# A hybrid HGRN2 / S5 layer on one core: projections of the unnormalised input, norms applied when an accumulator is emptied, head-norm chain at another priority, one reciprocal to four tokens

## The chip, the cores and the metric

The kernel runs on one core of one Trainium2 chip. The metric is the device time of one execution in microseconds; a kernel's time is the median of its timed runs. The engines are named as in the profile: PE (TensorE, matmul), PEld (its weight loads), DVE (VectorE), ACT (ScalarE), POOL (GpSimd), SP (the engine that issues most DMAs). L101 is line 101 of the kernel.

## The reference

One layer over 16 learned meta tokens and 256 tokens of the input (272 rows) of width 2048, in float32:

```python
xn = rmsnorm(h, norm_mix)                  # y = h * rsqrt(mean(h*h) + eps) * g, per row (token)
proj = xn @ w_in                           # 2048 x 5120
q, f_logit, i_in, g_out, u = split(proj)   # five times 1024 columns
# HGRN2, 8 heads, state 128x128, in chunkwise form:
f = lb + (1 - lb) * sigmoid(f_logit);  k = (1 - lb) * sigmoid(-f_logit);  q = silu(q);  v = i_in
S_t = diag(f_t) S_{t-1} + k_t v_t^T;       o_t = S_t^T q_t
o_hg = rmsnorm_per_head(o) * gain * silu(g_out)
# S5, 64 groups of 16 channels, 64 complex states each, diagonal recurrence along the tokens:
y = C (scan of ab * state + B u) + d * u;  y = gelu(y);  y = y * sigmoid(y @ w_glu + b_glu);  o_s5 = rmsnorm(y)
h = h + concat(o_hg, o_s5) @ w_out
# gated MLP of width 5632 with a causal convolution (width 3) on the gate branch, then a final rmsnorm
h = h + (silu(conv(n @ w_gate)) * (n @ w_up)) @ w_down     # n = rmsnorm(h, norm_ffn)
```

The factor rsqrt(mean(h*h) + eps) of the first norm belongs to a token, so it can be applied to the row of the input or to the finished row of the projection.

## The kernel before

**Layout.** Activations lie transposed: channels on the 128 partitions, tokens along the free axis. `xT` holds the input as 16 tiles of 128 x 272. Weights come in units of 1024 x 256, 1 MB by one DMA, in three rotating buffers `raw`; a unit consists of two halves, each 128 x 1024.

**Split products.** Every float32 product is made of rounded parts. For a weight half, ACT casts `whi` (L169) and DVE subtracts `wlo = raw - whi` (the helper `tt`, L92), each in three rotating buffers. The input is split likewise into `xh` and `xl`. `mm3` issues three matmuls for each pair of tiles: hi by high part (L193), hi by low part (L194), lo by high part (L195). A half of a projection serves 24 matmuls, and a chunk of 256 output columns takes 4 halves, 96 matmuls, into two accumulators `acc` (m = 0 and 1). Accumulators rotate through three PSUM buffers, so that the second accumulator of a chunk needs the first one of the chunk before to have been emptied.

**Stages.** (1) The head of the program: input rows arrive, PE transposes them into `xT`, ACT and DVE sum their squares (`row_rs`, L274), a small chain makes the factor of each token (`sqrt_rs`, L264), PE spreads it over the partitions (`rbp`, L298), and it lands in `rbs` (L307, L310). Then for each of the 16 tiles DVE forms `xn = xT * gm * rbs` (L101), ACT casts `xh` (L340), and DVE subtracts `xl`. The first two weight units are split in eight pieces of 512 columns, six of the subtracts on POOL; ten matmuls into `wps` (L312, 20 records in the trace) keep PE busy until the first `xh` is there. (2) 20 chunks of projections in the order u0 h0 u1 h1 u2 h2 u3 h3 g0 g1 g2 g3. `u` feeds the S5 part: per chunk two tiles `j`, each with its own weights (`s5_b`: B times small factors on POOL, copies `eb` and `cp` on ACT) and two scan passes (`s5_scan`: a rotation table W of six `stt`, products P, a sum on POOL, a scan, products, the sum `xo`), then a sum of products on PE (`yps`) and a GELU. `h` is three chunks (f, q, i) and the recurrence of two heads (`hg_group`, `hg_cross`); the tile `f` and later scratch of this recurrence share the one buffer `PP`. `g` is the output gate. (3) The head norms: squares of `oT` are summed by PE (`hps`, L862), a chain on DVE (`rsqrt`, then `hr`) makes eight factors, PE spreads each (`bps`, L893), and DVE multiplies, ACT casts `mh`, DVE subtracts `ml`, all beside the four chunks of `w_glu`. (4) `w_out` in 16 units, then the gated MLP and the last norm.

**Order.** A scheduler orders the instructions of each engine when the program is built: it takes what is ready in its own reckoning by priority (`pri`): splits of weights first (-4), then the emptying of accumulators (-3), then HGRN2 (-2), the rest by their place in the code, matmuls of weights last (+1). The result is one fixed list per engine; at run time each engine goes through its list in order, and an instruction that waits holds up all behind it.

## Time and profile before

| | |
|---|---|
| median of 3 runs (lowest, highest) | 1227.13 us (1224.62, 1233.77) |
| profiled execution: time, span | 1229.55 us, 1227.8 us |
| mean granted clock of PE | 0.993 |
| PE busy | 1205.0 us, 98% of the span |
| DVE busy | 892.9 us, 73% |
| ACT busy | 623.6 us, 51% |
| POOL busy | 83.2 us, 7% |
| moved by DMA | 210.66 MB, 172 GB/s |

The profiled execution lies 2.4 us above the median of the runs, and 1.75 us of its time lies outside the span. All times below that have a decimal place are microseconds from the start of this span. The page's list of busy tenths shows DVE at 9 from about 100 to 340 us and at 5 to 7 afterwards. A row of the trace's stages gives, after the stretch and its length, the busy time (and instructions) of PE, PEld, DVE, ACT and POOL, then the granted clock of PE, the busy share of the DMA engines and their GB/s. A row of the timeline gives start, duration, engine, line, operation, output <- inputs and shape, and in brackets the idle time ahead of it and what ended that. Engines are pipelined: DVE instructions that follow each other start about 0.08 us before the one ahead has ended, so a series costs its durations less 0.08 each.

### The profile page before, as it was taken

The page shows a single profiled execution, that of the slowest core. Times are in us where ns is not written, and L with a number is a line of the kernel's source. Part 1 is how long each engine was busy: PE and PEld are TensorE (multiplying, and loading weights), DVE is VectorE, ACT ScalarE, POOL GpSimd, SP SyncE. Part 2 cuts the span into 40 slices and gives each one's busy share as a digit, 9 for nine tenths or more (in the row PEclk, how much of TensorE's full clock was granted, in tenths as well). Part 3 has the DMA queues.
Part 4 walks back from the last instruction along what each step waited for, and adds up shares of the span by engine and source line. Part 5 has one row for each costly group of instructions (what it writes and reads, how often), then busy time and mean ns, then how long its engine had stood idle before and what let it go on. Part 6 is the DMA issues. An engine that isn't in the chain of part 4 may idle for free.

```text
span 1227.8 us, 21177 instructions
## 1 busy us (share of the span) xinstructions
PE 1205.0 (98%) x8531; PEld 1108.1 (90%) x8531; DVE 892.9 (73%) x1516; ACT 623.6 (51%) x1066; POOL 83.2 (7%) x102
## 2 busy tenths in 40 slices
PE   7989999999999999999999999999999999999997
PEld 6989999999989999999999999999999788888885
DVE  8988999999979778766666666765766555555554
ACT  6756667675655466444444444444443344444444
POOL 5231222111100000000000000000000000000000
PEclk9999999999999999999999999999999999999998
DMA  8544344434445555555655556565555545555552
GB/s 255 153 127 143 116 139 128 127 109 138 146 135 175 185 185 172 189 189 177 198 174 190 188 180 194 175 195 182 181 196 172 206 172 204 179 199 199 181 213 93
DMA packets 176289, 210.66 MB, mean 172 GB/s; under 512 B 14772, under 2 KB 168879, under 8 KB 170415
## 3 DMA queue, kind: packets, MB, share of 16 engines
q1 hardware_dynamic: 175871, 209.22, 52.4%
q8 instruction: 67, 1.10, 0.4%
q14 instruction: 31, 0.25, 0.1%
q0 software_dynamic: 320, 0.09, 0.0%
HBM read 206.08 MB, written 2.10 MB: 170 GB/s over the span
## 4 chain that ended last, share of the span: by engine, by line
PE 95%; DVE 2%; issue 1%; DMA 1%; ACT 1%; SPq 0%; POOL 0%; DVEq 0%; ACTq 0%; POOLq 0%
PE ua L976 13%; PE acc L193 10%; PE acc L194 9%; PE acc L195 9%; PE ga L193 7%; PE ga L195 7%; PE ga L194 7%; PE ua L982 7%; PE d L1047 7%; PE d L1049 7%; PE d L1048 7%; PE bu L623 1%; PE lps L753 1%; DVE xn L101 1%; DMA x<-in_x 0%
## 5 line engine op out<-in xcount | busy, mean ns | idle before, releaser
L92 DVE TENSOR_TENSOR wlo<-raw,whi 128x1024 fp32r<-128x1024 f32 (+1 forms) x376 | 462.0, 1229 | 288.6 <-ACT whi L169 238.7
L169 ACT CAST whi<-raw 128x1024 fp32r<-128x1024 f32 (+1 forms) x382 | 397.7, 1042 | 483.1 <-PE ga L194 157.4
L193 PE MATMUL ga<-fh,whi 128*128 128x258 f32 x704 | 198.9, 283 | 0.0
L195 PE MATMUL ga<-fh,wlo 128*128 128x258 f32 x704 | 198.1, 282 | 0.0
L194 PE MATMUL ga<-fl,whi 128*128 128x258 f32 x704 | 198.1, 282 | 0.0
L193 PE MATMUL acc<-xh,whi 128*128 128x272 f32 (+1 forms) x640 | 185.0, 293 | 3.1 <-ACT whi L169 3.1
L194 PE MATMUL acc<-xl,whi 128*128 128x272 f32 (+1 forms) x640 | 185.3, 291 | 1.9 <-DVE xl L92 1.9
L195 PE MATMUL acc<-xh,wlo 128*128 128x272 f32 (+1 forms) x640 | 183.2, 292 | 0.0
L194 PEld LDWEIGHTS ga<-fl,whi 128*128 128x128 f32 x704 | 133.6, 190 | 0.0
L193 PEld LDWEIGHTS ga<-fh,whi 128*128 128x128 f32 x704 | 133.1, 189 | 0.0
L195 PEld LDWEIGHTS ga<-fh,wlo 128*128 128x128 f32 x704 | 132.5, 189 | 0.0
L1048 PE MATMUL d<-whi,al 128*128 128x512 f32 x328 | 128.1, 391 | 0.0
L1047 PE MATMUL d<-whi,ah 128*128 128x512 f32 x328 | 127.4, 393 | 0.3 <-ACT ah L1040 0.3
L193 PEld LDWEIGHTS acc<-xh,whi 128*128 128x128 f32 x640 | 120.1, 189 | 7.1 <-ACT whi L169 3.3
L194 PEld LDWEIGHTS acc<-xl,whi 128*128 128x128 f32 x640 | 120.8, 189 | 4.7 <-DVE xl L92 2.8
L195 PEld LDWEIGHTS acc<-xh,wlo 128*128 128x128 f32 x640 | 119.6, 189 | 2.4 <-issue 1.0
L1049 PE MATMUL d<-wlo,ah 128*128 128x512 f32 x328 | 114.4, 390 | 0.0
L976 PE MATMUL ua<-fcxh,whi 128*128 128x512 f32 x352 | 96.6, 395 | 0.0
L976 PE MATMUL ua<-fcxl,whi 128*128 128x512 f32 x352 | 96.1, 394 | 0.0
L1047 PEld LDWEIGHTS d<-whi,ah 128*128 128x128 f32 x328 | 61.9, 189 | 13.3 <-ACT ah L1040 0.5
L1048 PEld LDWEIGHTS d<-whi,al 128*128 128x128 f32 x328 | 62.0, 189 | 12.9
L1049 PEld LDWEIGHTS d<-wlo,ah 128*128 128x128 f32 x328 | 61.9, 189 | 13.0
(417 smaller groups left out, 1897.7 us busy)
## 6 DMA issues: line engine op xcount, KB each, us to landing
raw<-in_w_ffn_gate SPq DMA_DIRECT2D x44, 1024.0 KB, 5.1
raw<-in_w_ffn_up SPq DMA_DIRECT2D x44, 1024.0 KB, 5.1
...
```

Of the source, the lines that this page charges most:

```text
L92: eng.tensor_tensor(out=dst, in0=a, in1=b, op=op)
L101: dve.scalar_tensor_tensor(out=dst, in0=a, scalar=s, in1=b, op0=op0, op1=op1, **kw)
L169: act.copy(out=hi[:, c], in_=raw[:, hf, c])
L193: pe.matmul(accs[m], lh, xh[:, n0:n1], start=first, stop=False)
L194: pe.matmul(accs[m], lh, xl[:, n0:n1], start=False, stop=False)
L195: pe.matmul(accs[m], ll, xh[:, n0:n1], start=False, stop=end)
L623: return pe.matmul(bus[i][:, ri], bt[h, 2 * ri + q0 // 2], R[h, q0 // 2], start=True, stop=True)
L976: pe.matmul(accs[m].rearrange("p a n -> p (a n)"), hi[:, k * 256 + m * 128:k * 256 + m * 128 + 128], c.rearrange("p a n -> p (a n)"), star ...
L982: pe.matmul(accs[m][:, 0], lo[:, k * 256 + m * 128:k * 256 + m * 128 + 128], c[:, 0], start=False, stop=(kt == KD - 1), skip_group_check=True)
L1047: pe.matmul(dps[t][n], ah[:, tk], hi, start=False, stop=False, skip_group_check=True)
L1048: pe.matmul(dps[t][n], al[:, tk], hi, start=False, stop=False, skip_group_check=True)
L1049: pe.matmul(dps[t][n], ah[:, tk], lo, start=False, stop=end, skip_group_check=True)
```

## The change

- The projections take the input without its row factor. `xh` is ACT's `xT * gm` rounded (one activation with a scale per partition), `xl` is one DVE instruction, `xT * gm - xh`. `xn` is gone. `gm` no longer carries the factor -0.5, and `norm_mix` is loaded ahead of the input.
- The first two weight units and the 16 tiles are split in eight steps, each tied to follow the one before: `whi` and `wlo` of 512 columns, then two tiles. All eight subtracts are on DVE; the ten matmuls into `wps` are gone.
- The row factors are made as before, most of it at a later priority, into three columns `rcol`; they are spread by PE after the chunk u0 into a PSUM buffer of the accumulators, and ACT copies them to `rbs`.
- The row factor is applied when an accumulator is emptied: `ysb` (was a copy on ACT), `f`, `q` and `g` by a `tt` on DVE with `rbs`, followed by sigmoids from SBUF; `v` by ACT's copy with a scale.
- In `hg_group`, the reciprocal of 512 elements per partition is replaced by one of 128 (one to a block of four tokens), three `tt` of 128, one of 384 and an ACT copy.
- In `s5_scan`, the axes of `P` are stored in another order, and the sum is made in place instead of in a tile `m`.
- `c_kinds(1)`, small work for the S5 part, stands in chunk u2 instead of after u1.
- The chain of the head norms (`hrs`, `hr`, `ht`) has an offset of -3 within its -2, which sets it ahead of the splits of weights.

```diff
     early = []
-    deps = []
+    units = []
 
     def wunit(src):
         with pri(-4):
-            return wsplit(early.pop(0), (dve, pool), 2, deps.pop(0)) if early else wsplit(wload(src))
-
-    def wsplit(raw, eng=(dve, dve), parts=1, dep=None):
+            return units.pop(0) if units else wsplit(wload(src))
+
+    def wsplit(raw):
         res = []
-        n = 1024 // parts
         for hf in range(2):
             hi = wsp.tile([128, 1024], F32R, tag="whi", name="whi")
             lo = wsp.tile([128, 1024], F32R, tag="wlo", name="wlo")
-            if dep is not None and dep[hf] is not None:
-
-                act.copy(out=hi[:, 0:1], in_=dep[hf])
-            for i in range(parts):
-                c = slice(i * n, (i + 1) * n)
-                act.copy(out=hi[:, c], in_=raw[:, hf, c])
-                tt(lo[:, c], raw[:, hf, c], hi[:, c].bitcast(F32), SUB, eng[max(hf, i)])
+            act.copy(out=hi, in_=raw[:, hf])
+            tt(lo, raw[:, hf], hi.bitcast(F32), SUB)
             res.append((hi, lo))
...
-    rbp = [pmm.tile([128, NM + 128], F32, tag="mm", name=f"rbp{b}") for b in range(2)]
-    rbs = xin.tile([128, T], F32, name="rbs")
+    rbs = s5p.tile([128, T], F32, name="rbs")
...
-    rm = row_rs(xm, NM, 1, "rm")
-    rb = [None, None]
+    gm = prm.tile([128, KD], F32, name="gm")
+    gps = ptp.tile([128, KD], F32, tag="tp", name="gps")
+    pe.transpose(gps, nrow, ident[0:KD, 0:KD])
+    dve.tensor_copy(out=gm, in_=gps)
-        rb[b] = row_rs(xt[b], 128, 2, f"rb{b}")
-        if b == 0:
-            spread(rm, NM, rbp[0][:, 0:NM])
-            spread(rb[0], 128, rbp[0][:, NM:])
-            act.copy(out=rbs[:, 0:NM + 128], in_=rbp[0])
-        else:
-            spread(rb[1], 128, rbp[1][:, 0:128])
-            dve.tensor_copy(out=rbs[:, NM + 128:T], in_=rbp[1][:, 0:128])
-            for _ in range(NWARM2):
-                pe.matmul(wps, ident, rbs[:, NM + 128:T], start=True, stop=True)
...
-            gm = prm.tile([128, KD], F32, name="gm")
-            gps = ptp.tile([128, KD], F32, tag="tp", name="gps")
-            pe.transpose(gps, nrow, ident[0:KD, 0:KD])
-            ts(gm, gps, -0.5, MUL)
+    last = None
+    for p in range(8):
+        u, hf, c = p // 4, p // 2 % 2, slice(512 * (p % 2), 512 * (p % 2) + 512)
+        if p % 4 == 0:
+            units.append([])
+        if p % 2 == 0:
+            units[u].append([wsp.tile([128, 1024], F32R, tag=t, name=t) for t in ("whi", "wlo")])
+        hi, lo = units[u][hf]
+        raw = early[u][:, hf, c]
+
+        def split():
+            i = act.copy(out=hi[:, c], in_=raw)
+            tt(lo[:, c], raw, hi[:, c].bitcast(F32), SUB)
+            return i.ins
+
+        if last is None:
+            wi = split()
+        else:
+            with tc.issue_after(last):
+                wi = split()
+        with tc.issue_after(wi):
+            for kt in (2 * p, 2 * p + 1):
+                last = act.activation(out=xh[:, kt], in_=xT[:, kt], func=AF.Identity, scale=gm[:, kt:kt + 1]).ins
+                stt(xl[:, kt], xT[:, kt], gm[:, kt:kt + 1], xh[:, kt].bitcast(F32), MUL, SUB)
+
+    rcol = s5p.tile([128, 3], F32, name="rcol")
+    rb = [row_rs(xt[0], 128, 2, "rb0")]
+    with pri(0.5):
+        rb += [row_rs(xt[1], 128, 2, "rb1"), row_rs(xm, NM, 1, "rm")]
+    for i, n in enumerate((128, 128, NM)):
+        ts(rcol[:n, i:i + 1], rb[i], -0.5, MUL)
...
-    for kt in range(KD):
-        xn = xin.tile([128, T], F32, tag="xn", name="xn", bufs=4)
-        stt(xn, xT[:, kt], gm[:, kt:kt + 1], rbs, MUL, MUL)
-        act.copy(out=xh[:, kt, :], in_=xn)
-        tt(xl[:, kt, :], xn, xh[:, kt, :].bitcast(F32), SUB)
-    tc.cur_priority += 900000
-    deps[:] = [(None, xh[:, 0, 0:1].bitcast(F32)), tuple(xh[:, i, 0:1].bitcast(F32) for i in (3, 6))]
...
     def s5_u(j, ps):
-        pv = ps.rearrange("p (k s) -> p s k", s=2)
-        act.copy(out=ysb[:, j], in_=pv)
+        pv, rv = (a.rearrange("p (k s) -> p s k", s=2) for a in (ps, rbs))
+        tt(ysb[:, j], pv, rv, MUL)
...
-            tt(P[:, :, :, i * TH:(i + 1) * TH], win(i), bus[i].unsqueeze(1).to_broadcast([128, 2, 2, TH]), MUL)
-        m = s5w.tile([128, 2, 2 * TH], F32, tag="m", name="m", bufs=1)
-        tt(m, P[:, :, 0], P[:, :, 1], ADD, pool)
+            tt(P[:, :, :, i * TH:(i + 1) * TH].rearrange("p b a n -> p a b n"), win(i), bus[i].unsqueeze(1).to_broadcast([128, 2, 2, TH]), MUL)
+        m = P[:, 0]
+        tt(m, m, P[:, 1], ADD, pool)
...
-        tt(P, win(None), m.unsqueeze(1).to_broadcast([128, 2, 2, 2 * TH]), MUL)
+        tt(P.rearrange("p b a n -> p a b n"), win(None), m.unsqueeze(1).to_broadcast([128, 2, 2, 2 * TH]), MUL)
         xo = s5w.tile([128, 2, 2, TH], F32, tag="xo", name="xo", bufs=2)
-        tt(xo.rearrange("p r j k -> p r (j k)"), P[:, :, 0], P[:, :, 1], ADD)
+        tt(xo.rearrange("p r j k -> p r (j k)"), P[:, 0], P[:, 1], ADD)
...
         for m in range(2):
+            tt(f[:, m], accs[m], rbs, MUL)
+        fact(k, f, AF.Sigmoid, scale=-1.0)
+        fact(f, f, AF.Sigmoid)
+        for m in range(2):
             h = h0 + m
-            fact(k[:, m], accs[m], AF.Sigmoid, scale=-1.0)
-            fact(f[:, m], accs[m], AF.Sigmoid)
             fact(f[:, m], f[:, m], AF.Identity, scale=lbc[:, 1, h:h + 1], bias=lbc[:, 0, h:h + 1])
         ts(f, f, FLOOR, MAX)
         return f, k
         q = hgp.tile([128, 2, NQ], F32, tag="q", name="q")
...
         for m in range(2):
-            fact(sg[:, m], accs[m], AF.Sigmoid)
-            stt(q[:, m], accs[m], lbc[:, 1, h0 + m:h0 + m + 1], sg[:, m], MUL, MUL)
+            tt(q[:, m], accs[m], rbs[:, T0:T], MUL)
+        fact(sg, q, AF.Sigmoid)
+        for m in range(2):
+            stt(q[:, m], q[:, m], lbc[:, 1, h0 + m:h0 + m + 1], sg[:, m], MUL, MUL)
         return q
 
...
-        act.copy(out=v, in_=tp)
+        for b in range(2):
+            fact(v.rearrange("p (m b) e -> p b m e", b=2)[:, b], tp.rearrange("p (m b) e -> p b m e", b=2)[:, b],
+                 AF.Copy, scale=rcol[:, b:b + 1])
         tp = ptp.tile([128, 4, 128], F32, tag="tp", name="vtp")
         for m in range(2):
             pe.transpose(tp[0:NM, m], iv[:, m, 0:NM], ident)
-        act.copy(out=vm[0:NM], in_=tp[0:NM, 0:2])
+        fact(vm[0:NM], tp[0:NM, 0:2], AF.Copy, scale=rcol[0:NM, 2:3])
         return v
 
     def hg_g(h0, accs):
         sg = hgp.tile([128, 2, NQ], F32, tag="sg", name="sg")
         for m in range(2):
-            fact(sg[:, m], accs[m], AF.Sigmoid)
-            stt(gs[:, h0 + m], accs[m], vcol[:, V_HG + h0 + m:V_HG + h0 + m + 1], sg[:, m], MUL, MUL)
+            tt(gs[:, h0 + m], accs[m], rbs[:, T0:T], MUL)
+            fact(sg[:, m], gs[:, h0 + m], AF.Sigmoid)
+            stt(gs[:, h0 + m], gs[:, h0 + m], vcol[:, V_HG + h0 + m:V_HG + h0 + m + 1], sg[:, m], MUL, MUL)
 
     def hg_group(h0, f, k, q, v):
         SP = hgp.tile([128, 2, T], F32, tag="SP", name="SP")
...
+
+        qt = hgp.tile([128, 2, 256], F32, tag="sg", name="qt")
+        f4, s4, q4, r4 = (z.rearrange("p m (n t) -> p m n t", t=4)
+                          for z in (f[:, :, NM:T], SP[:, :, NM:T], q[:, :, 2:NQ], qt))
+        tt(r4[:, :, :, 0], s4[:, :, :, 0], f4[:, :, :, 3], MUL)
+        dve.reciprocal(out=r4[:, :, :, 0], in_=r4[:, :, :, 0])
+        tt(r4[:, :, :, 1], r4[:, :, :, 0], s4[:, :, :, 0], MUL)
+        tt(r4[:, :, :, 2], r4[:, :, :, 1], f4[:, :, :, 2], MUL)
+        tt(r4[:, :, :, 0:3], r4[:, :, :, 0:3], q4[:, :, :, 0:3], MUL)
+        act.copy(out=r4[:, :, :, 3], in_=q4[:, :, :, 3])
         widen(2)
         kt = kts[0]
-        qt, rv = (hgp.tile([128, 2, 256], F32, tag=t_, name=n_) for t_, n_ in (("sg", "qt"), ("qm", "rv")))
-        dve.reciprocal(out=rv, in_=SP[:, :, NM:T])
         tt(kt.rearrange("p (m b) t -> p m (b t)", b=2), k[:, :, NM:T], SP[:, :, NM:T], MUL)
-        tt(qt, q[:, :, 2:NQ], rv, MUL)
         ps = psc.tile([128, 4, 128], F32, tag="sc", name="dps")
         for m in range(2):
...
 
     def do_u(c):
         accs = chunk(w_in, 16 + c)
+        if c == 0:
+            rbp = pmm.tile([128, T], F32, tag="mm", name="rbp")
+            spread(rcol[0:NM, 2:3], NM, rbp[:, 0:NM])
+            for b in range(2):
+                spread(rcol[:, b:b + 1], 128, rbp[:, NM + 128 * b:NM + 128 * (b + 1)])
+            act.copy(out=rbs, in_=rbp)
         with pri(-3):
             for m in range(2):
                 s5_u(2 * c + m, accs[m])
+        if c == 2:
+            c_kinds(1)
         for m in range(2):
             s5_tile(2 * c + m, *s5_split(2 * c + m), *s5_b(2 * c + m))
-        if c == 1:
-            c_kinds(1)
 
     def do_h(g):
         accs = chunk(w_in, 4 + g)
...
-        hrs = rsqrt(hgp, hps, [128, NQ], 1.0 / 128, "rh", tags=("iv", "qm", "v"))
-
-        hr = hgp.tile([128, NQ], F32R, tag="SP", name="hr")
-        ht = hgp.tile([128, NQ], F32, tag="iv", name="ht")
-        act.copy(out=hr, in_=hrs)
-        ts(ht, hr.bitcast(F32), misc[:, 26:27], MUL)
-        stt(hr, hrs, misc[:, 27:28], ht, MUL, ADD)
+        with pri(-3):
+            hrs = rsqrt(hgp, hps, [128, NQ], 1.0 / 128, "rh", tags=("iv", "qm", "v"))
+
+            hr = hgp.tile([128, NQ], F32R, tag="SP", name="hr")
+            ht = hgp.tile([128, NQ], F32, tag="iv", name="ht")
+            act.copy(out=hr, in_=hrs)
+            ts(ht, hr.bitcast(F32), misc[:, 26:27], MUL)
+            stt(hr, hrs, misc[:, 27:28], ht, MUL, ADD)
     ssum = tlp.tile([128, NQ], F32, name="ssum")
     for c in range(4):
         u = [(wunit(colunit(w_glu, 0, c)), 0)]
```

More of the change, by code (lines that the diff above doesn't have):

```diff
@@ L39 @@
 NWARM = 8
-NWARM2 = 10
 LATE = 1.003
@@ L234, in hymba_kernel @@
     sp.dma_start(out=xm, in_=meta)
+    sp.dma_start(out=nrow, in_=norm_mix.rearrange("o (r c) -> (o r) c", c=128))
     HD = D // 2
@@ L250, in hymba_kernel @@
             sp.dma_start(out=xt[b][:, hf * HD:(hf + 1) * HD], in_=x[b * 128:(b + 1) * 128, hf * HD:(hf + 1) * HD])
-        if b == 0:
-            sp.dma_start(out=nrow, in_=norm_mix.rearrange("o (r c) -> (o r) c", c=128))
     early.append(wload(colunit(w_in, 0, U0), 2))
```

2 lines of the change are left out of this document (removed).

## Prediction

> **What bounds the kernel now.** I read the page first, then busy time by stage, then who waits for whom.
>
> ```profile
> PE 1205.0 (98%) x8531; PEld 1108.1 (90%) x8531; DVE 892.9 (73%) x1516; ACT 623.6 (51%) x1066; POOL 83.2 (7%) x102
> ```
>
> PE is busy for 1205.0 of 1227.8 us. The change takes no matmul of weights away, so it can win only what PE waits (22.8 us in all) or runs at a lower clock. By stage:
>
> ```profile
> 20.00:41.20 21.20, 18.88 (x143) 17.65 (x142) 20.40 (x59) 13.69 (x30) 7.80 (x10) 1.00 0.56 155
> 50.40:100.00 49.60, 45.31 (x378) 43.85 (x377) 43.77 (x113) 27.83 (x60) 18.02 (x24) 0.97 0.47 141
> 100.00:340.00 240.00, 239.98 (x2150) 224.81 (x2149) 236.95 (x414) 156.42 (x382) 43.84 (x43) 1.00 0.42 131
> 340.00:378.40 38.40, 38.40 (x322) 34.91 (x322) 28.86 (x56) 22.18 (x42) 0.00 (x0) 1.00 0.43 138
> ```
>
> From 100 to 340 PE never waits, but DVE is busy for 236.95 of 240 us: two engines are full at once, and PE stays ahead only while DVE's list is never late. That row decides most of what follows. PE's waits lie earlier:
>
> ```profile
> PE acc L193 <- ACT whi L169: 3.1, 1, 3.1
> PE acc L194 <- DVE xl L92: 1.9, 2, 1.8
> ```
>
> **The change, part by part.** Sums are made against the profiled execution (1229.55 us, 2.4 above the median); the forecast is taken back by 2.4 at the end.
>
> *The head.* DVE's list before, from its first split of weights on (`rb1y` is a row factor, `rbs` all of them spread):
>
> ```order
> L92 TENSOR_TENSOR wlo<-raw,whi 128x512
> L101 SCALAR_TENSOR_TENSOR rb1y<-rb1t,rb1y 128x1
> L322 COPY xT<-xps 128x4x128 x2
> L310 COPY rbs<-rbp_155 128x128
> L96 TENSOR_SCALAR gm<-gps 128x16
> L101 SCALAR_TENSOR_TENSOR xn<-xT,gm,rbs 128x272 x4
> L92 TENSOR_TENSOR xl<-xn,xh 128x272 x3
> L101 SCALAR_TENSOR_TENSOR xn<-xT,gm,rbs 128x272 x3
> ```
>
> and after, from the squares of the meta tokens (`rmss`) on:
>
> ```order
> L100 SCALAR_TENSOR_TENSOR junk_139,rmss<-xm 16x1024
> L275 TENSOR_REDUCE rb1st<-rb1ss 128x1
> L305 COPY xT<-xps 128x4x128
> L275 TENSOR_REDUCE rmst<-rmss 16x1
> L97 TENSOR_SCALAR rb1v<-rb1st 128x1
> L91 TENSOR_TENSOR wlo<-raw,whi 128x512
> L97 TENSOR_SCALAR rmv<-rmst 16x1
> L100 SCALAR_TENSOR_TENSOR xl<-xT,gm,xh 128x272 x2
> L91 TENSOR_TENSOR wlo<-raw,whi 128x512
> L100 SCALAR_TENSOR_TENSOR xl<-xT,gm,xh 128x272 x2
> ```
>
> The row factors have left the path, and a tile costs DVE one instruction, not two. The prices:
>
> ```profile
> 10.54 0.63 ACT L89 ACTIVATE junk<-x 128x512 bf16<-128x512 f32 x1 [0.61 <-DMA x<-in_x]
> 13.03 0.68 DVE L92 TENSOR_TENSOR wlo<-raw,whi 128x512 fp32r<-128x512 f32 x1
> 23.77 0.49 DVE L101 SCALAR_TENSOR_TENSOR xn<-xT,gm,rbs 128x272 f32<-128x272 f32 x1
> 25.16 1.04 ACT L474 COPY scb<-sca 128x1024 f32<-128x1024 f32 x1
> 29.03 1.05 ACT L169 CAST whi<-raw 128x1024 fp32r<-128x1024 f32 x1
> L101 DVE SCALAR_TENSOR_TENSOR junk<-xm 16x1024 bf16<-16x1024 f32 x1 | 1.2, 1211 | 3.1 <-DMA xm<-in_meta_tokens 3.1
> ```
>
> The input is there at 10.5 in both. The first `wlo` moves from 13.03 to about 14.2 (behind the meta squares, 1.21 - 0.08). A step of DVE is then 0.60 + 2 x 0.41 = 1.42; eight make 11.4, small instructions of the row factors between them about 1.3 (an estimate), so the last `xl` ends near 27. PE's 12 matmuls of that step end u0 near 28.5. In ACT's list two copies `scb`, `sca` (1.04 each), a `whi` (1.05) and `rbs` (0.4) stand behind the last `xh`, and the first accumulator of h0 needs the buffer that `rbs` empties: h0 starts near 30.2. Before, at 41.2:
>
> ```profile
> 20.00:41.20 21.20, 17.45 (x120) 15.56 (x120) 0.00 (x0) 0.39 (x1) 1.00 0.56 155
> ```
>
> 120 matmuls `acc`, 24 beyond u0, and 1.4 us of other PE work (18.88 - 17.45). The same point comes after at 30.2 + 3.0 + 1.4 = 34.6, or 35 with a little for waits: **-6** (-3 if h0 waits longer for its first splits, -8 if ACT's copies come earlier).
>
> *The wait at 80 us.* The 3.1 us of the waits is this:
>
> ```profile
> 73.08 6.76 POOL L92 TENSOR_TENSOR bt<-br,abr 128x64 f32<-128x64 f32 x1 [12.62 <-DMA br<-in_s_b_re]
> 79.59 0.28 DVE L96 TENSOR_SCALAR pw<-pt 128x32 f32<-128x32 f32 x1
> 81.18 0.94 ACT L552 COPY eb<-br 64x256 f32<-64x256 f32 x2 [7.05 <-POOL br L92]
> 83.36 0.39 PE L193 MATMUL acc<-xh,whi 128*128 128x272 f32 x1 [3.06 <-ACT whi L169]
> 85.00:88.40 3.40, 3.40 (x18) 3.40 (x18) 3.40 (x5) 0.84 (x3) 3.11 (x4) 0.50 1.02 337
> ```
>
> A product of 64 elements takes POOL 6.76 us and ends as DVE's run of instructions with two tensor inputs ends at 79.6; ACT's copy `eb` waits for it, the `whi` queued behind that is late, PE stands 3.06, and the clock is then 0.50 for 3.4 us (another 1.7). It is a chance meeting of lists that all move, so I take it as gone: **-4.8** (0 if it comes back). The Trainium skill (SBUF — State Buffer, "SBUF: two separate sides") says that a DVE instruction with two SBUF inputs and a GpSimd instruction that reads SBUF exclude each other, the holder for its whole instruction; by that POOL would have waited for one instruction of at most 1.2 us and nothing would be won here, while the row shows a dozen.
>
> *DVE's list in the full stretch.* I count weight halves from 0. Between the subtract of half 26 and that of half 60, before:
>
> ```profile
> 117.41 1.21 DVE L92 TENSOR_TENSOR wlo<-raw,whi 128x1024 fp32r<-128x1024 f32 x1
> 271.22 1.21 DVE L92 TENSOR_TENSOR wlo<-raw,whi 128x1024 fp32r<-128x1024 f32 x1
> 117.40:271.20 153.80, 153.80 (x1384) 143.02 (x1385) 151.68 (x263) 104.93 (x264) 32.16 (x37) 1.00 0.42 128
> 123.06 0.39 PE L195 MATMUL acc<-xh,wlo 128*128 128x258 f32 x1
> 273.74 0.29 PE L194 MATMUL acc<-xl,whi 128*128 128x272 f32 x1
> 273.86 0.29 PE L195 MATMUL acc<-xh,wlo 128*128 128x272 f32 x1
> ```
>
> PE uses half 26 at 123.06, 4.4 after DVE has it, and half 60 at 273.86, only 1.4 after; DVE idles 2.1 of the 153.8. Half 26 was followed in DVE's list by one scan pass (`W`, `P`) and leftovers of HGRN2 (`qm`, `PP`):
>
> ```order
> L92 TENSOR_TENSOR wlo<-raw,whi 128x1024
> L92 TENSOR_TENSOR qm<-qx,PP 128x2x128
> L92 TENSOR_TENSOR P<-W,bu 128x4x136 x2
> L101 SCALAR_TENSOR_TENSOR W<-W,pw,tmp 128x2x17 x2
> L96 TENSOR_SCALAR PP<-PP 128x544
> ```
>
> Now nine rows follow half 26, and then these (two scan passes, HGRN2, and the emptying of f):
>
> ```order
> L91 TENSOR_TENSOR P<-W,bu 128x2x2x136 x2
> L100 SCALAR_TENSOR_TENSOR W<-W,pw,tmp 128x2x17 x2
> L91 TENSOR_TENSOR PP<-PP 128x2x2x64
> L91 TENSOR_TENSOR kx<-k,SP 128x256
> L91 TENSOR_TENSOR qm<-q,PP 128x2x128
> L91 TENSOR_TENSOR qx<-q,PP 128x256
> L100 SCALAR_TENSOR_TENSOR W<-W,pw,tmp 128x2x34 x2
> L612 SCALAR_TENSOR_TENSOR P<-r2t,P 128x544
> L91 TENSOR_TENSOR qm<-qx,PP 128x2x128
> L91 TENSOR_TENSOR P<-W,P 128x2x2x272
> L100 SCALAR_TENSOR_TENSOR W<-W,pw,tmp 128x2x68
> L91 TENSOR_TENSOR PP<-acc,rbs 128x272 x2
> ```
>
> The S5 passes have moved forward, and the emptying `PP<-acc,rbs`, for which PE's second accumulator of q waits, stands behind them. In all 314 DVE instructions lie between the two subtracts instead of 262. The prices:
>
> ```profile
> L92 DVE TENSOR_TENSOR P<-W,bu 128x544 f32<-128x544 f32 x22 | 14.7, 709 | 0.0
> L92 DVE TENSOR_TENSOR P<-W,m 128x1088 f32<-128x1088 f32 x10 | 12.9, 1289 | 0.0
> L608 DVE TENSOR_TENSOR_SCAN m<-r2t,m 128x544 f32<-128x544 f32 x10 | 12.8, 1278 | 0.0
> L726 DVE RECIPROCAL rv<-SP 128x512 f32<-128x512 f32 x3 | 10.0, 3342 | 0.0
> L92 DVE TENSOR_TENSOR xo<-P 128x544 f32<-128x544 f32 x11 | 8.0, 723 | 0.0
> L101 DVE SCALAR_TENSOR_TENSOR W<-W,pw,tmp 128x34 f32<-128x34 f32 x22 | 7.0, 353 | 0.0
> L101 DVE SCALAR_TENSOR_TENSOR W<-W,pw,tmp 128x68 f32<-128x68 f32 x20 | 4.8, 273 | 0.0
> L92 DVE TENSOR_TENSOR ysb<-ysb,gq 128x258 f32<-128x258 f32 x5 | 2.1, 411 | 0.0
> 35.20 0.34 DVE L421 RECIPROCAL den<-den 128x32 f32<-128x32 f32 x1
> ```
>
> All less 0.08. S5, moved forward: four `P<-W,bu` 2.5, four wide products 4.8, three scans 3.6, three `xo` 1.9, fourteen `W` at 0.19 to 0.27 3.5: 16.3. Evictions: 14 at 0.33 (a `tt` of 258), 4.6. Reciprocals: three of 3.26 go; two of 128 elements come, which I put at 0.94 - 0.08 by the line through 0.34 at 32 and 3.34 at 512; with their small products (1.0 a group) less the two old ones (0.6): -7.3. HGRN2 work of about 2.4 more stands ahead of half 60 now. Sum +16. Against this DVE has 2.1 idle and 1.4 of lead at the end; at the start at most one more half of lead than before, 4.4 (150.8 / 34), less likely none. PE's own list is the same here. So PE waits 8.1 to 12.5 by half 60, and what DVE then lacks behind half 60 gives nothing back, as PE is the bound there. I take **+9.5**, nearer the end with lead, since `xn` is gone before half 26. A wait of over 3 us can cost the lower clock as at 85 us: **+1** (0 to 3.4).
>
> *The head norms.* PE's list before, at the first `bps` (the factors `hr` spread by `hsel`), among the GLU's matmuls (`gh`) and 52 ahead of the first of w_out (`mh`, `ml`):
>
> ```order
> L193 MATMUL acc<-gh_4662,whi 128x258
> L194 MATMUL acc<-gh_4662,whi 128x258
> L893 MATMUL bps<-hr,hsel 128x258 x2
> L195 MATMUL acc<-gh_4662,wlo 128x258
> L193 MATMUL acc<-gh_4663,whi 128x258
> ```
>
> and after, at the end of the GLU:
>
> ```order
> L188 MATMUL acc<-gh_4632,wlo 128x258
> L918 MATMUL bps<-hr,hsel 128x258 x4
> L186 MATMUL acc<-mh,whi 128x258 x3
> L918 MATMUL bps<-hr,hsel 128x258 x2
> L187 MATMUL acc<-ml,whi 128x258
> ```
>
> All eight `bps` now stand behind the last GLU matmul, in spite of the earlier priority.
>
> ```profile
> 372.39 0.75 DVE L92 TENSOR_TENSOR oT<-oT,bps 128x258 f32<-128x258 f32 x2
> L895 ACT CAST mh<-oT 128x258 fp32r<-128x258 f32 x8 | 2.9, 402 | 0.1
> ```
>
> `mh` is there 0.4 + 0.42 + 0.40 = 1.2 after that matmul; the first `ml` has on DVE two `oT` (0.7), a subtract of weights (1.13), four `tt` (1.4) and itself (0.34) ahead: 0.4 + 3.6 = 4.0. PE has 9 matmuls of 0.12, 1.1, to fill that with: **+3** (0 if DVE has its weights' subtract behind it by then and the GLU ends late, 4.5 if the later `ml` hold PE too). It is idle a quarter of the time there (28.86 of 38.4).
>
> Sum: -6 - 4.8 + 9.5 + 1 + 3 = +2.7, 1232.3 profiled, **1230** as a median.
>
> **The rivals.** *The full stretch absorbs it.* If DVE's lead is large and the regrouped S5 instructions run a little shorter, only the one emptying behind half 26 costs PE, some 3: -6 - 4.8 + 3 + 3 = -4.8, 1222.4. For it: leads of 4.4 exist. Against: 1.4 at half 60. *POOL is starved again* (slower). POOL sums every S5 pass and scales every `s5_b`; with DVE never resting it meets the 6.76 of above again. It decides where DVE's run of two-input instructions exceeds about 4 us ahead of an `eb` that has a `whi` behind it; one such place at 4.8 gives 1234.7, two 1239.5. Against: of the eight `s5_b` one did so before. *The clock.* `wps` now gone kept PE busy ahead of the first `acc`:
>
> ```profile
> 16.31 4.12 PE L312 MATMUL wps<-rbs,ident 128*128 128x128 f32 x20 [0.31 <-DVE rbs L310]
> ```
>
> If u0, fed in pieces, ran at 0.50 throughout, its 96 matmuls would take 24, not the 13.5 from 15 to 28.5, less the 1.7 between u0's end and h0: +8.8, 1238.7. The Trainium skill (TensorE: Matmul & The Clock Gate, "What's actually happening") makes half clock the default that a window of activity lifts. PE is fed at 1.46 in 1.42 us of each step, hence unlikely. *Neither DVE nor the head norms cost anything*: -10.8, 1216.
>
> **How the numbers follow.** Forecast 0.40 (its own range 1224 to 1237), absorbed 0.25, POOL starved 0.17, clock 0.06, no cost 0.12. The range that leaves out 2 in 10 is 1216 to 1240. One per cent is about what a measurement can tell here: faster (under 1214.9) takes half the last case, 0.07; slower (over 1239.4) most of POOL's and a tail, 0.14.
>
> **What would show it.** First `acc` of h0 near 30; no 3 us wait near 80; between 100 and 275 waits of PE for DVE (`PP`, `wlo`) of 8 to 12 us, DVE at 99%; about 3 us before the first `ml`. A PE with no waits there proves the ledger wrong; one below 0.9 clock in u0 the clock's rival right.

## The result, and the profile after

The changed kernel takes **1236.37 us** (median of 15 runs, 1234.78 to 1238.66), the kernel before 1226.07 us (15 runs, 1223.04 to 1233.77): a ratio of **1.0074, 95% interval 1.0059 to 1.0089**. It is slower by some 9 us. The profiled execution of after takes 1235.32 us with a span of 1233.4; that of before, from which the prediction was made, took 1229.55 with 1227.8.

Busy times hardly move (the page of after, part 1):

```profile
PE 1205.2 (98%) x8511; PEld 1106.4 (90%) x8511; DVE 889.1 (72%) x1552; ACT 626.0 (51%) x1051; POOL 78.9 (6%) x96
```

So the question is again where PE waits. The moment when PE first uses the `wlo` of a weight half (counted from 0, as in the prediction, and by number: eight matmuls with `wlo` to a half, so it measures how far PE has come with the weights even where it takes halves in another order) shows where the two part, in us from the start of the span:

| first use of half | before | after | difference | gained or lost since the row above |
|---|---|---|---|---|
| 4 (first of h0) | 37.2 | 30.8 | -6.4 | -6.4 |
| 18 | 91.5 | 78.1 | -13.4 | -7.0 |
| 25 | 119.2 | 105.1 | -14.1 | -0.7 |
| 26 | 123.1 | 118.7 | -4.4 | +9.7 |
| 60 | 273.9 | 279.5 | +5.6 | +10.0 |
| 87 (last of the GLU) | 375.7 | 378.2 | +2.5 | -3.1 |
| 90 (in w_out) | 385.2 | 392.2 | +7.0 | +4.5 |
| 100 | 414.5 | 421.8 | +7.3 | +0.3 |
| end of span | 1227.8 | 1233.4 | +5.6 | -1.7 |

After is 14 us ahead at half 25. It loses 19.7 us between halves 25 and 60, half of that from one half to the next, and 4.5 us at the end of the GLU.

This table does not count PE's small matmuls (those of S5, HGRN2 and the norms), and some of these have moved as well. So here is the same difference by what PE did: its waits (the stretch less its busy time), what the lower clock cost (half of its busy time where the trace has the clock at 0.50), and the rest, work at full clock:

| from half to half | longer by | waits | lower clock | work |
|---|---|---|---|---|
| start to 4 | -6.5 | -1.3 | -0.1 | -5.0 |
| 4 to 25 | -7.6 | -4.4 | -1.7 | -1.6 |
| 25 to 60 | +19.8 | +9.6 | +3.8 | +6.3 |
| 60 to 87 | -3.2 | 0.0 | 0.0 | -3.2 |
| 87 to 90 | +4.6 | +1.6 | +1.6 | +1.4 |
| 90 to end | -1.4 | 0.0 | -1.7 | +0.3 |
| whole span | +5.7 | +5.5 | +1.9 | -1.7 |

Between halves 25 and 60 PE has 78 matmuls more than in before, and between 60 and 87 it has 53 fewer. These rows are before's two stretches, then after's:

```profile
119.15:273.86 154.71, 154.71 (x1393) 143.93 (x1392) 152.59 (x264) 105.69 (x263) 32.16 (x37) 1.00 0.40 123
273.86:375.66 101.80, 101.78 (x895) 94.89 (x894) 91.86 (x165) 59.14 (x127) 9.73 (x4) 1.00 0.45 143
...
105.06:279.54 174.48, 164.86 (x1471) 149.35 (x1469) 171.41 (x321) 116.56 (x294) 42.36 (x40) 0.97 0.35 109
279.54:378.16 98.62, 98.62 (x842) 93.41 (x841) 80.35 (x151) 51.48 (x96) 5.74 (x2) 1.00 0.45 146
```

So about a third of the 19.7 us is work that only stands elsewhere in PE's list; 9.6 us are waits and 3.8 us lower clock. The stretches of after (from 100 to 340 us, before had PE at 239.98 of 240 us and DVE at 236.95):

```profile
20.00:41.20 21.20, 21.20 (x171) 21.02 (x170) 18.15 (x62) 14.50 (x25) 0.00 (x0) 1.00 0.84 237
...
100.00:340.00 240.00, 230.38 (x2053) 212.31 (x2053) 230.53 (x431) 151.21 (x360) 48.10 (x42) 0.98 0.38 120
340.00:391.00 51.00, 49.42 (x370) 45.30 (x369) 36.32 (x71) 27.41 (x50) 0.00 (x0) 0.97 0.45 145
103.00:118.00 15.00, 10.39 (x76) 8.58 (x76) 15.00 (x31) 7.43 (x24) 3.21 (x2) 0.78 0.12 36
```

In the first row PE has no gap and the full clock. From 100 us on it now stands still for 9.6 of the 240 us. The last row is the place itself: from 103 to 118 us PE is busy for 10.39 of 15 us at a clock of 0.78, and DVE for all 15. PE's timeline there: the first accumulator of q has used the weights of halves 24 to 26 by 106.3, the second begins at 115.9:

```profile
106.15 0.28 PE L188 MATMUL acc<-xh,wlo 128*128 128x258 f32 x1
...
111.18 1.02 PE L794 MATMUL xps<-qx,kx 128*128 128x128 f32 x4 [1.04 <-DVE qx L91]
...
114.76 1.20 PE L800 MATMUL mps<-qm,km 128*128 128x258 f32 x2 [2.56 <-ACT sx L796]
...
115.91 0.58 PE L186 MATMUL acc<-xh,whi 128*128 128x258 f32 x1
...
118.69 0.28 PE L188 MATMUL acc<-xh,wlo 128*128 128x258 f32 x1
```

From 106.4 to 115.9 PE has only small products (`lps`, `xps` and `mps` of HGRN2, `bu` of S5) and waits in between; no weight matmul runs. The waits stand ahead of the small products; the second accumulator of q follows `mps` in PE's list. DVE in the same time, from the subtract of half 26 to the emptying of f:

```profile
102.83 1.21 DVE L91 TENSOR_TENSOR wlo<-raw,whi 128x1024 fp32r<-128x1024 f32 x1
103.97 1.28 DVE L91 TENSOR_TENSOR P<-W,P 128x1088 f32<-128x1088 f32 x1
...
108.02 1.34 DVE L91 TENSOR_TENSOR P<-W,bu 128x544 f32<-128x544 f32 x2
...
112.44 1.28 DVE L612 TENSOR_TENSOR_SCAN P<-r2t,P 128x544 f32<-128x544 f32 x1
113.64 0.39 DVE L91 TENSOR_TENSOR qm<-qx,PP 128x256 f32<-128x256 f32 x1
113.96 1.28 DVE L91 TENSOR_TENSOR P<-W,P 128x1088 f32<-128x1088 f32 x1
115.16 0.35 DVE L100 SCALAR_TENSOR_TENSOR W<-W,pw,tmp 128x136 f32<-128x136 f32 x1
115.43 0.77 DVE L91 TENSOR_TENSOR PP<-acc,rbs 128x272 f32<-128x272 f32 x2
```

f's accumulators have been complete since the end of half 23. They are emptied at 115.43, for the emptying writes the buffer `PP`, which f of the group before holds until `qm<-qx,PP` has read it at 113.64. PE's second accumulator of q needs the bank that f's first one holds; that is empty at 115.86, and the accumulator starts at 115.91. PE's waits (the view of who waits for whom) are spread thin over this place and the same place of the later groups (the two for `PP` lie at 193.9 and 268.2), and none of 3 us is left near 80 us:

```profile
PE mps L800 <- ACT sx L796: 2.6, 1, 2.6
PE acc L186 <- DVE PP L91: 2.3, 2, 1.2
...
PE mps L800 <- ACT W L587: 1.2, 1, 1.2
...
PE xps L794 <- DVE qx L91: 1.0, 1, 1.0
```

The end of the GLU, in PE's timeline (`bps` spreads the head norms, `mh` and `ml` are the normed heads in two parts):

```profile
380.80 0.40 PE L918 MATMUL bps<-hr,hsel 128*128 128x258 f32 x2
381.60 0.72 PE L918 MATMUL bps<-hr,hsel 128*128 128x258 f32 x2 [0.40 <-DVE oT L91]
382.95 0.62 PE L186 MATMUL acc<-mh,whi 128*128 128x258 f32 x3 [0.64 <-ACT mh L920]
...
384.92 0.58 PE L187 MATMUL acc<-ml,whi 128*128 128x258 f32 x1 [0.25 <-DVE ml L91]
385.30 0.42 PE L188 MATMUL acc<-mh,wlo 128*128 128x258 f32 x1
```

The waits are short, but the matmuls then take 0.42 instead of 0.28 us until 387.7. All eight `bps` stand behind the GLU's last matmul (380.68); in before, four of them stand ahead of it.

### The profile page after: what moved, and what is told of

It reads as the page before. It is cut to its first block, busy times and chain, and to the rows that moved or that the text cites. A ratio compares the mean times of both kernels' runs of the same rounds, so it can differ in the third digit from the quotient of the medians.

```text
span 1233.4 us, 21146 instructions
## 1 busy us (share of the span) xinstructions
PE 1205.2 (98%) x8511; PEld 1106.4 (90%) x8511; DVE 889.1 (72%) x1552; ACT 626.0 (51%) x1051; POOL 78.9 (6%) x96
## 4 chain that ended last, share of the span: by engine, by line
PE 81%; DVE 14%; issue 2%; ACT 1%; DMA 1%; POOL 0%; SPq 0%; DVEq 0%; ACTq 0%; POOLq 0%
PE ua L1001 13%; PE ga L186 7%; PE ga L188 7%; PE ga L187 7%; PE ua L1007 7%; PE d L1072 6%; PE d L1074 6%; PE d L1073 6%; PE acc L186 6%; PE acc L187 6%; PE acc L188 6%; DVE wlo L91 3%; DVE P L91 2%; DVE W L100 2%; DVE P L612 1%
## 5 line engine op out<-in xcount | busy, mean ns | idle before, releaser
L91 DVE TENSOR_TENSOR wlo<-raw,whi 128x1024 fp32r<-128x1024 f32 (+1 forms) x382 | 464.3, 1216 | 291.1 <-ACT whi L162 241.6
L162 ACT CAST whi<-raw 128x1024 fp32r<-128x1024 f32 x374 | 393.0, 1051 | 470.8 <-PE ga L187 157.6
```

What stands on the lines that cost most here:

```text
L91: eng.tensor_tensor(out=dst, in0=a, in1=b, op=op)
L162: act.copy(out=hi, in_=raw[:, hf])
```

## The experiments

All times are medians; intervals are of the ratio to the runs of before on the same chip. The columns with halves are from each profiled execution, as in the table above.

| kernel | us | ratio (95%) | half 25 | 26 | 60 | 87 | 90 | 100 |
|---|---|---|---|---|---|---|---|---|
| after | 1236.4 | 1.0059 to 1.0089 | 105.1 | 118.7 | 279.5 | 378.2 | 392.2 | 421.8 |
| f in space of its own | 1231.5 | 1.0024 to 1.0057 | 105.7 | 108.6 | 258.5 | 365.0 | 382.2 | 418.6 |
| no row factors | 1222.9 | 0.9957 to 0.9990 | 106.2 | 114.5 | 270.0 | 369.1 | 379.7 | 408.6 |
| full reciprocal | 1238.1 | 1.0061 to 1.0118 | 106.3 | 116.3 | 269.8 | 374.2 | 390.9 | 422.4 |
| early sums | 1231.8 | 1.0034 to 1.0058 | 105.8 | 119.8 | 278.6 | 379.0 | 388.6 | 417.9 |
| own space and early sums | **1222.6** | 0.9954 to 0.9980 | 105.4 | 108.2 | 258.1 | 365.2 | 379.2 | 408.1 |
| these, full reciprocal | 1228.2 | 0.9999 to 1.0036 | 106.0 | 110.2 | 255.5 | 375.0 | 384.5 | 413.9 |
| f through k, early sums | 1224.5 | 0.9989 to 1.0006 | 106.1 | 114.6 | 265.3 | 370.8 | 382.3 | 411.5 |
| before, reciprocal and P | 1232.2 | 1.0028 to 1.0060 | 113.3 | 122.0 | 272.6 | 372.9 | 387.4 | 416.7 |
| before, early sums | 1226.4 | 1.0001 to 1.0027 | 121.5 | 125.4 | 276.3 | 379.7 | 388.9 | 418.4 |
| before, reciprocal, P and both | 1227.1 | 0.9992 to 1.0017 | 114.3 | 121.4 | 275.1 | 374.0 | 383.2 | 412.4 |

**1. f in space of its own.** Two theories stood against each other: that the place of f's emptying costs the time, or that DVE's total work does. The tile `gs` (the gates) is first written at 311.9 us in after, behind half 68, so f of the second to fourth group can be emptied there. No instruction is added.

```diff
+        fe = gs.rearrange("p h n -> p (h n)")[:, 0:544].rearrange("p (m t) -> p m t", m=2) if h0 else f
         for m in range(2):
-            tt(f[:, m], accs[m], rbs, MUL)
-        fact(k, f, AF.Sigmoid, scale=-1.0)
-        fact(f, f, AF.Sigmoid)
+            tt(fe[:, m], accs[m], rbs, MUL)
+        fact(k, fe, AF.Sigmoid, scale=-1.0)
+        fact(f, fe, AF.Sigmoid)
```

> The second to fourth f are emptied into space of their own (the tile gs, not yet in use), everything else is as after the change. Theory 1 (the place of the emptying): PE loses its time because the emptying of f needs the buffer PP, which is free only when the cross terms of the group before have read it, and these stand far back in DVE's list. Then PE's wait behind half 26 goes (PE first uses the wlo of half 26 at 105 to 111 us instead of 118.7), half 60 is reached at 265 to 271 instead of 279.5, and what is gained is in part given back between halves 87 and 100, since S5 and the head norms then end later relative to PE: 1226 to 1231 us. Theory 2 (DVE's total work sets the time of the stretch, whatever stands where): half 60 stays within 3 us of 279.5 and the time is 1234 to 1238 us.

1231.47 us, 4.9 less than after and half a us above theory 1's range. The first emptyings in DVE's timeline, at 101.43 where they were at 115.43:

```profile
101.43 0.43 DVE L91 TENSOR_TENSOR gs<-acc,rbs 128x272 f32<-128x272 f32 x1
103.36 0.43 DVE L91 TENSOR_TENSOR gs<-acc,rbs 128x272 f32<-128x272 f32 x1
```

Half 26 is reached 10.1 us earlier and half 60 at 258.5, 21.0 us earlier: more than the 8 to 15 expected. Halves 26 to 60 take 149.9 us, as in before (150.8). Between halves 25 and 60 PE waits 1.6 us instead of 9.6, and the 3.8 us of lower clock are gone: these losses hang on that buffer, with all the multiplications by the row factors still on DVE. The rest of the 21.0 us is not won but moved: S5 stands further back, with 271 instead of 314 DVE instructions between the subtracts of halves 26 and 60, and PE has 76 fewer small matmuls there. By half 100, 17.8 of the 21.0 us are given back, 8.0 of them in new waits. The windows, and the waits of PE in that kernel:

```profile
100.00:340.00 240.00, 237.87 (x2170) 223.11 (x2169) 239.04 (x441) 156.52 (x367) 49.61 (x42) 1.00 0.42 132
340.00:391.00 51.00, 41.97 (x294) 37.12 (x295) 42.31 (x97) 27.15 (x54) 0.00 (x0) 0.95 0.34 109
```

```profile
PE bps L919 <- DVE hr L100: 4.1, 1, 4.1
...
PE acc L187 <- DVE ml L91: 2.2, 1, 2.2
PE acc L188 <- DVE wlo L91: 2.0, 4, 0.8
PE acc L186 <- DVE xT L91: 2.0, 1, 2.0
```

DVE is now full for 239.04 of 240 us, and PE waits at the end of the GLU instead, 9 us in the second window. The place sets where PE waits; something else sets when w_out can go on.

**2. No row factors.** f, q, g and u are taken out of their accumulators by ACT and DVE as before the change, without the product with `rbs`; the norm's factor of each token is left out there.

```diff
-            tt(f[:, m], accs[m], rbs, MUL)
-        fact(k, f, AF.Sigmoid, scale=-1.0)
-        fact(f, f, AF.Sigmoid)
+            fact(k[:, m], accs[m], AF.Sigmoid, scale=-1.0)
+            fact(f[:, m], accs[m], AF.Sigmoid)
```

> The projections f, q, g and u are emptied without being multiplied by the row factors, as before the change (f and u on ACT alone); the norm's factor of each token is so left out of these, and the emptyings on DVE go (32 instructions, some 11 us of DVE's time, 5.6 us of it between halves 26 and 60). Theory 1 (place): most of the wait behind half 26 goes with them, since ACT takes f out with nothing of DVE's list ahead but the buffer: half 26 at 110 to 114 us, 1222 to 1228 us. Theory 2 (DVE's total): half 60 comes earlier by just what DVE saves, 5 to 7 us, and the time is 1229 to 1232 us.

1222.88 us, 13.5 less than after, at the lower end of theory 1. Half 26 comes at 114.5, not quite in the range: ACT waits for the same buffer. Half 60 comes 9.5 us earlier, 5.3 of it after half 26, near the 5.6 us of DVE's work that the expectation puts there. So the row factors at the emptying cost 13.5 us for some 11 us of DVE's time, more than the whole head wins.

**3. Full reciprocal**, the one part undone that should spare DVE time.

```diff
+        dve.reciprocal(out=rv, in_=SP[:, :, NM:T])
+        tt(qt, q[:, :, 2:NQ], rv, MUL)
-        tt(r4[:, :, :, 0], s4[:, :, :, 0], f4[:, :, :, 3], MUL)
-        dve.reciprocal(out=r4[:, :, :, 0], in_=r4[:, :, :, 0])
...
```

> After the change with the one reciprocal per block of four undone: 512 elements to a reciprocal again. DVE has 2.2 us more per group, 6 us more between halves 26 and 60. Theory 2 (DVE's total): half 60 is reached 6 us later, 1241 to 1244 us. Theory 1 (place): in DVE's list the emptying of f stands 19 rows behind half 26 instead of 24, so the wait there gets no longer; the head norms come later, as DVE ends its stretch later: 1234 to 1242 us. In the prediction the reciprocals give 7.3 us of DVE's time back.

1238.13 us, 1.8 more, with intervals that overlap, so in the time itself no difference is shown. Theory 2 missed: half 60 is reached 9.7 us *earlier* with more work on DVE, and between halves 25 and 60 PE waits 6.1 us instead of 9.6. Fewer DVE instructions stand ahead of f's emptying, which is the 19th row behind the subtract of half 26 here and the 24th in after. It is all lost again behind: halves 60 to 87 take 104.4 us (98.7 in after), 87 to 90 16.7 (14.0), 90 to 100 31.5 (29.6), with 7.0 us of waits in these (1.6 in after).

**4. The same parts on before.** The reciprocal and the layout of P alone, put into the kernel before:

> Before the change, with only the one reciprocal to a block of four and the new layout of P. DVE has 7 us less between halves 26 and 60 of the stretch in which PE does not wait. Prediction's picture (PE is the bound there, DVE runs just behind): no gain from DVE's time; S5 moves forward by one pass and all eight bps now stand behind the last GLU matmul, which costs 2 to 4 us between halves 87 and 90: 1226 to 1231 us. Rival (DVE is the bound of the stretch): 1219 to 1222 us.

1232.23 us, 6.4 *more* than before, and above both ranges. Less work on DVE made the kernel slower: S5 goes forward, halves 25 to 26 take 8.7 us (3.9 in before), 87 to 90 take 14.5 (9.5). These are the two places of after, without the new place of the norm. Of the first, only 0.9 us are a wait; the rest is 76 small matmuls more. From half 25 to 90 PE waits 4.3 us here and not at all in before, and loses 1.7 us more to the lower clock.

**5. Early sums.** In after 12 us lie between the last heads' `oT` (done at 351.2) and the norms' first step on DVE (363.2); the trace of ACT, PE and DVE:

```profile
350.78 0.37 ACT L809 COPY oT<-ops 128x258 f32<-128x258 f32 x1 [2.53 <-PE ops L808]
353.55 0.64 PE L886 MATMUL hps<-sq,misc 128*32 128x258 f32 x6
...
362.56 0.62 PE L886 MATMUL hps<-sq,misc 128*32 128x258 f32 x2
363.21 0.43 DVE L97 TENSOR_SCALAR rhv<-hps 128x258 f32<-128x258 f32 x1 [1.04 <-PE hps L886]
```

`hps` sums the squares of all eight heads in the one bank that the cross terms use too, so even the first heads' squares come after them.

```diff
-        hps = psc.tile([128, NQ], F32, tag="sc", name="hps")
-        for h in (0, 2, 4, 6, 1, 3, 5, 7):
+        hps = ptp.tile([128, NQ], F32, tag="tp", name="hps")
+        for h in range(8):
```

> After the change, with one thing moved: the head norms' sums of squares (hps) get the accumulation bank of btp and vtp instead of the one they share with the cross terms, and the squares are taken in the order of the heads, so that six of the eight no longer wait for the last heads' outputs. After the change 13 us lie between the last oT (351.2 us) and the end of hps (363.2). Theory 3 (the wait at the end of the GLU is the chain of the head norms, which starts late because DVE ends the last group's cross terms late): hps ends some 8 us earlier, the first bps comes at about 372 instead of 380.8 us, halves 87 to 90 take 9.5 to 11 us instead of 14.0, 1231 to 1234 us. Rival (what PE waits for there is DVE's work behind half 90, wlo, oT and ml, not the start of the chain): 87 to 90 stays at 13 to 14 us and the time at 1235 to 1238 us.

1231.8 us, 4.6 less than after: theory 3. `rhv` starts at 357.7 instead of 363.2, 5.5 us earlier rather than 8, and the first `bps` at 376.2 rather than 372; that was enough. Halves 87 to 90 take 9.6 us: four of the `bps` stand ahead of the GLU's last matmul again, and the 1.6 us of waits and 1.6 us of lower clock are gone.

> Before the change, with the head norms' sums moved in the same way. PE does not wait at the end of the GLU there (halves 87 to 90 in 9.5 us), so nothing can be won: 1223 to 1228 us, no change. A time under 1220 us would say that the move helps for another reason than the wait.

1226.38 us beside 1225.77: no gain where PE does not wait, as expected.

**6. Own space and early sums together.**

> Both together: f of the second to fourth group emptied into space of its own, and the head norms' sums in another bank. With the first alone PE was 21 us ahead at half 60 (258.5 instead of 279.5) and 3.2 ahead at half 100, having waited 4.1 us for hr, 2.2 for ml and 2.0 for xT, each followed by half clock. Theory 3: the chain of the head norms starts 8 us earlier, so these waits go for the most part: half 100 at 404 to 410 us, 1217 to 1224 us. Theory 2 (DVE's total work up to the head norms sets the time, it is full to 342 us in that run): what one wait gives the next takes, half 100 at 415 to 419 us, 1228 to 1232 us.

**1222.56 us, 13.8 less than after**, and faster than before (0.9967, 0.9954 to 0.9980). The parts alone gave 4.9 and 4.6. PE waits 28.2 us of the whole span in after, 27.1 with the own space, 25.5 with the early sums and 19.8 with both: the own space alone moves the wait from behind half 25 to the end of the GLU, and there the early sums take it away. Half 60 in PE's timeline, and DVE's first step of the head norms, 14 us earlier than in after:

```profile
258.08 0.29 PE L188 MATMUL acc<-xh,wlo 128*128 128x272 f32 x1
```

```profile
349.41 0.43 DVE L97 TENSOR_SCALAR rhv<-hps 128x258 f32<-128x258 f32 x1
```

```profile
100.00:340.00 240.00, 238.40 (x2142) 222.15 (x2142) 237.89 (x440) 156.09 (x366) 49.71 (x42) 1.00 0.41 129
340.00:391.00 51.00, 49.78 (x392) 46.40 (x391) 42.12 (x86) 26.65 (x50) 0.00 (x0) 0.97 0.45 141
```

PE stands still for 2.8 us of the 291; half 100 comes at 408.1, in theory 3's range.

**7. Does DVE's total matter once the places are right?** The same kernel with the full reciprocals.

> The kernel with both (f in space of its own, the sums of the head norms in another bank; 1222.6 us) with the reciprocals undone, 512 elements each again: 2.2 us of DVE's work more in each of four groups, 8.8 us in all, up to the head norms. If only places in the lists matter (theory 1), PE does not feel it: 1221 to 1225 us. If DVE's work up to the head norms sets the time as soon as no wait for a place is left (theory 2; DVE is busy for 159.93 of 160 us from 100 to 260 and for 40.00 of 40 to 300 there), 5 to 9 us come on top: 1227 to 1232 us.

1228.19 us, 5.6 more for 8.8 us of DVE's work: theory 2. The new wait of PE, and the window that pays:

```profile
PE acc L186 <- ACT gh L869: 3.6, 1, 3.6
```

```profile
340.00:375.00 35.00, 30.81 (x251) 29.07 (x250) 30.81 (x61) 17.58 (x37) 1.37 (x1) 0.90 0.33 101
```

`gh` is S5's last output, the input of the GLU. DVE's list up to S5's end and the head norms is a bound of its own, and the cheap reciprocal is worth 5.6 us there, though together with the layout of P it won nothing in before.

> Before the change, with the one reciprocal to a block of four and the layout of P, f emptied into space of its own, and the head norms' sums moved. The reciprocal and layout alone took 1232.2 us, 6.4 more than before, with 4.8 us more between halves 25 and 26 and 5.0 more between 87 and 90. Theory 3: both losses are such waits, made by instructions of DVE's list that stand elsewhere, and both go: 1219 to 1226 us. Rival (less work on DVE just moves S5 forward and costs PE in other places too): 1228 to 1233 us.

1227.13 us beside 1225.77: the 6.4 us lost in experiment 4 come back to 1.4 (interval -1.0 to +2.1 us), at the upper edge of theory 3 (1219 to 1226) and just outside it. The second wait is gone (87 to 90 in 9.2). Halves 25 to 26 still take 7.2 us, with the same 0.9 us of waits as in experiment 4. In all, PE waits 0.9 us between halves 25 and 90 instead of 4.3, but nothing is won against before.

**8. f through k.** The two multiplications write `k`, read for the last time six rows before `PP`.

```diff
-            tt(f[:, m], accs[m], rbs, MUL)
-        fact(k, f, AF.Sigmoid, scale=-1.0)
-        fact(f, f, AF.Sigmoid)
+            tt(k[:, m], accs[m], rbs, MUL)
+        fact(f, k, AF.Sigmoid)
+        fact(k, k, AF.Sigmoid, scale=-1.0)
```

> After the change with the sums of the head norms moved (1231.8 us), and f emptied by the same two multiplications into k, which is read for the last time some rows earlier in the cross terms than PP; the sigmoids then go from k to PP and from k to k. No space is added. Theory 1: the wait behind half 26 becomes shorter by what lies between the last reading of k and that of PP in DVE's list (6 rows, some 3 to 5 us) and does not go: half 26 at 111 to 116 us (119.8 without it, 108.2 with space of its own), 1223 to 1229 us. Rival (the buffer does not matter, the two emptyings are late because DVE is): half 26 stays at 118 to 120 and the time at 1230 to 1233 us.

1224.46 us, 7.3 less than with early sums alone; half 26 at 114.6. It comes 5.3 us earlier, about what the rows between take, as theory 1 has it, and PE's waits between halves 25 and 60 fall from 9.5 to 4.8 us.

**9. The kernel before, looked at again.** The prediction won 4.8 us at a wait of PE near 80 us that the profile of before shows.

> The kernel before, unchanged, looked at again. Its executions so far have a mean granted clock of either 0.996 to 0.997 or 0.992 to 0.994; the one that the prediction is made from (1229.55 us, 0.993) is of the second kind and 3.5 us above the median. Theory A: the wait of 3.1 us near 80 us belongs to the kernel and stands in every execution: half 16 to half 18 takes 12 to 14 us whatever the clock. Theory B: it is a matter of some tens of nanoseconds between POOL and DVE and is there in some executions only: in one at 0.996 or more it is missing, half 16 to 18 takes 6.5 to 8 us, and the time is 1223 to 1226 us. By theory B the prediction's 4.8 us could be won in the profiled execution but not in the median.

> The same kernel once more, as a second look, with the same two theories: the wait near 80 us in every execution (half 16 to 18 in 12 to 14 us), or only in those with a mean clock of 0.992 to 0.994.

1226.63 and 1227.76 us; halves 16 to 18 take 7.6 us in both (12.6 in the first profile). The wait is missing in both, at a mean clock of 0.993 and of 0.996: it is there in some executions only, and the clock does not tell which (theory B, less its sign; the times lie 0.6 and 1.8 us above its range). The stretch in the profile of before, and in the first of the two:

```profile
70.00:95.00 25.00, 20.71 (x164) 19.86 (x163) 20.83 (x43) 11.71 (x25) 11.92 (x12) 0.93 0.41 121
```

```profile
70.00:95.00 25.00, 23.76 (x217) 23.04 (x216) 25.00 (x48) 14.66 (x33) 10.92 (x12) 1.00 0.51 155
```

In the profile of before with early sums (1233.11 us, the slowest of that kernel's twelve runs) it is there again:

```profile
74.45 6.92 POOL L92 TENSOR_TENSOR bt<-br,abr 128x64 f32<-128x64 f32 x1 [12.55 <-DMA br<-in_s_b_re]
...
84.89 0.60 PE L193 MATMUL acc<-xh,whi 128*128 128x272 f32 x1 [3.12 <-ACT whi L169]
```

## Why the prediction was right or wrong

The time lies in the range (1216 to 1240) and in the case "within 1%", 6.4 us above the forecast of 1230. Of the 6.4, 3.0 are in the profiled time (1235.3 against a sum of 1232.3), and 3.4 in taking it back to a median.

- **The head, -6: right as a place, too much as a gain.** -6.4 in the two profiles, with PE at full clock and without a gap from 20 to 41 us. The two further looks at before have half 4 at 39.4 and 40.4, so there it is rather more. But 5.0 of the 6.5 us are work that PE does not have there, and only the ten `wps` are gone for good: 2.4 us at full clock (an estimate: 4.1 us, of which 3.4 at a clock of 0.50). The other small matmuls come behind half 25.
- **The wait at 80 us, -4.8: right for the profile, wrong for the median.** It is gone after the change; it is also absent in both further looks at before. The step that failed is "the forecast is taken back by 2.4 at the end": the profiled execution of before carried a chance wait that the sum counted as a gain, while the profile of after lies 1.05 us *below* its median.
- **DVE's list, +9.5: the size right, the reason only in part.** Between halves 25 and 60 PE waits 9.6 us more. Between the subtracts of halves 26 and 60 DVE is busy for 169.95 us, 18.3 more than in before, where the ledger had 16; the S5 passes, the 14 emptyings and the reciprocals are there as it counted them:

```profile
102.83:275.79 172.96, 163.34 (x1457) 147.83 (x1457) 169.95 (x315) 115.56 (x293) 42.36 (x40) 0.97 0.36 110
```

  The step from this surplus to "PE waits 8.1 to 12.5 by half 60" came out, but it is no law of the kernel: experiment 1 keeps every instruction and the waits fall to 1.6, experiment 3 adds work and they fall to 6.1. What counted in these runs is which instructions stand ahead of f's emptying. The prediction had the rows in its hands: it quoted `PP<-acc,rbs` standing behind S5 and named q's second accumulator as waiting for it, and then priced a total and not that place, where 4.6 of the 9.6 us fall. Only 3.0 of the 9.6 end with `PP` or `wlo`, which its signs named; most of the others end with steps of HGRN2 on ACT and DVE (`sx`, `qx`, `S`).
- **The lower clock, +1: too small.** From 111.4 us it is at 0.50 for 6.8 us and from 268.4 for 3.4, which cost 3.8 us. This and the head's small matmuls are why the profiled sum came out 3.0 short; 1.3 us more won up to half 25, and 1.7 us of lower clock that after does not have near the end, go the other way.
- **"What DVE then lacks behind half 60 gives nothing back": right here.** PE does not wait between halves 60 and 87 in either kernel; the 3.2 us of the table are work done earlier. With the place repaired, the opposite holds: DVE's total comes due at the end of the GLU (experiments 1 and 7).
- **The head norms, +3: the size right (1.6 us of waits, 1.6 of lower clock), the reason half.** The place was right: all eight `bps` behind the last GLU matmul. Priced were the subtract, the `oT` and the `tt` ahead of the first `ml`. What decides is when the chain starts: early sums take all of it away without touching these rows. "In spite of the earlier priority" was right in a way not meant: built without that priority, the kernel has the same list for every engine, so that edit did nothing. Nor does the later place of the second `c_kinds` change the order of operations on any engine.
- **The rivals.** *Absorbed* and *no cost* are refuted by the same trace (9.6 us of waits). *Clock* is refuted as priced: u0 does not run at 0.50 throughout, but 3.4 us of its start do (15.8 to 19.2), so the mean over 14 to 30 us is 0.89, and the sign "below 0.9 clock in u0" is met without the 8.8 us. Before has 3.4 us at 0.50 in the same place, on `wps`. *POOL is starved again*: it is (6.59 us, below), but no `eb` with a `whi` behind it stood there, and it cost PE nothing.

That the size of the waits came out is in part luck, as the same instructions in another order give 1.6 us.

Left open: the buffer and the S5 rows ahead of the emptying come and go together in these lists; S5 held back with the buffer left as it is wasn't tried. The 1.7 us behind half 100 are 3.4 us at a clock of 0.50 from 979.3 on, which of the two profiles only that of before has; PE waits 1.8 us at that place in both, so why it is in one of them stays open.
